# The depthwise convolution's matrix share moved to ScalarE and GpSimd, and the scan's products issued in pairs

## The chip, the cores and the metric

The kernel runs on one core of a Trainium2 chip (trn2). A core has PE (the TensorE matrix engine), VectorE (DVE in the profile), ScalarE (ACT), GpSimd (POOL) and SyncE (SP), which issues most DMAs; each works through its own list of instructions in order, and they wait for each other by semaphores. The metric is the device time of one execution in us, the median of several runs.

## The reference, cut to what matters

Three layers run over a sequence of 256 tokens with 2048 features. The change lies in the first layer, which has two branches over one projection: a depthwise convolution of 31 taps, and a grouped state-space scan.

```
proj = rmsnorm(x) @ w_in
glu  = a[:, :1024] * sigmoid(a[:, 1024:])             # a = proj[:, :2048]
y    = sum over k of w_dw[k] * padded(glu)[t + k]     # 31 taps for each of 1024 channels
y    = silu(layernorm(y + b_dw)) @ w_pw
bu   = einsum('gph,bsgh->bsgp', b_bar, ug)            # scan: 64 groups of 16 channels, 64 states
s[t] = lam_bar * s[t - 1] + bu[t]
out  = Re(c @ s) + d_skip * u ; gelu, two projections, a gate
```

...then come an output projection, a layer of retrieved experts, and a second block with a delta-rule mixer and banded attention. They are not touched.

## The kernel before

Features lie on the 128 partitions, the 256 tokens along the free dimension, so the 1024 channels of the convolution are 8 chunks of 128x256, and its input glu, its output cy and its weights dw lie in SBUF. Weights of the large products are fetched as strips of 128x1024 fp32. `strips` (L162, L163) splits a strip into wh (a ScalarE cast) and wl (a VectorE difference); `dual` (L175, L176) multiplies each by the operand, a product of 512 columns and one of 256, and `fold` (L181, L182) adds the two halves of the sum. One output block of 128 features is 16 such pairs over two strips; it is read out of PSUM by a VectorE product (`evict`, L342).

Side work is written as generators and stepped between the pairs of a block; STEP says how many steps a block takes. The scheduler then orders each engine's list, with the casts and splits of the strips at high priority, so the list differs from the order written. The first layer runs its blocks so: 8 blocks for the scan's input u, 16 blocks for glu, 32 gate blocks (about 178 to 440 us in the profile), 16 half blocks of conv_w_out, and so on.

- `ssm_scan` (L574 to L662) runs from the u blocks into conv_w_out. It handles 32 groups of two. For a group g: two fp32 products into a PSUM tile bu (L611, L612), VectorE work of 256 or 512 columns (L614 to L628), a difference and a sum of 128x256 on GpSimd (L630, L631), and three groups later the output product (`outp`, L639), which writes 32 partitions of yp. The weights of L611 and L612 have 128 rows, all but 32 of them zero. Three buffers t1 carry the groups.
- `conv` (L665 to L675) does five chunks of the convolution on VectorE, in gate blocks, one multiply-add of 128x256 for each tap and chunk (L674): first three chunks, then two.
- `conv_pe` (L704 to L736) does the other three on PE: for each tap ScalarE scales the identity twice (L728, L729) into a diagonal matrix's high and low part, and `dual` multiplies them by the split input (L722, L723): 93 pairs into cps, three folds.
- `conv_norm` (L677 to L702) follows when all eight chunks are there.

Of the kernel before, what the change touches and what calls it, by code (L numbers as in the profile page):

```python
# [10 lines left out]
F32 = mybir.dt.float32  # L11
F32R = mybir.dt.float32r
# [5 lines left out]
ALU = mybir.AluOpType  # L18
# [6 lines left out]
W2 = 512  # L25
STEP = (6, 2, 2.25, 3.7, 3, 2)
GRATE = 0.2
# [12 lines left out]
GLAG = 2  # L40
CDVE = ((0, 1, 2), (3, 4))
CPE = (5, 6, 7)
DLAG = 2
TSTEP = 2
# [72 lines left out]
class K:  # L117
# [189 lines left out]
    def mixers(self):  # L307
        nc, tc, I = self.nc, self.tc, self.I
        with ExitStack() as ctx:
# [68 lines left out]
            side = Side()  # L378
            side.add(self.ssm_scan(c1, prm, u, y, cc, wk, (sw[:, 7168:8192], cw[:, 4864:5888]), cw[:, 5888:8192]))
            evict(u[:, 2, :], p2)  # L380
# [24 lines left out]
            c4 = E(ExitStack())  # L405
            dg = c4.enter_context(tc.tile_pool(name="dg", bufs=DLAG + 1))
            side3 = Side()
            side3.add(self.conv_pe(c1, dg, glu, cy, dw, CPE))
            norm = self.conv_norm(sm, cy, *cx)
# [163 lines left out]

    def ssm_scan(self, c1, prm, u, y, cc, wk, bms, wb):  # L574

# [11 lines left out]
        tabs = [area(wk, 4 + 2 * i) for i in range(4)]  # L587
        t1s, t2s = (area(wk, 12), area(wb, 0), area(wb, 5)), (area(wk, 14), area(wb, 2), area(wb, 7))

# [12 lines left out]
        def scan(g):  # L602
            j, q = g // 4, g % 4
            t1, t2, t = t1s[g % 3], t2s[g % 3], tabs[g % 4]
            bm = bms[j % 2].rearrange("p (q k c) -> p q k c", q=4, k=2)
# [3 lines left out]
            sin = t[:, 1:2, :].to_broadcast([P, 2, T])  # L609
            bu = self.ips.tile([P, 512], F32, name="bu", tag="i").rearrange("p (k t) -> p k t", k=2)  # L610
            nc.tensor.matmul(bu[:, 0, :], lhsT=bm[:, q, 0, :], rhs=u[:, j, :], start=True, stop=True)  # L611
            nc.tensor.matmul(bu[:, 1, :], lhsT=bm[:, q, 1, :], rhs=u[:, j, :], start=True, stop=True)  # L612
            yield
            V.tensor_tensor(out=t1, in0=bu, in1=cos, op=ALU.mult)  # L614
            yield
# [18 lines left out]
        def outp(g, yp):  # L634
            q = g % 4
            t1 = t1s[g % 3]
            yo = yp[32 * q : 32 * q + 32, :]
            for n in range(2):
                nc.tensor.matmul(yo, lhsT=cc[:, g, n, :], rhs=t1[:, n, :], start=n == 0, stop=n == 1, tile_position=(0, 32 * q))  # L639

# [3 lines left out]
        for tick in range(4 * 35):  # L644
            if tick % 4 == 0:
                g = tick // 4
                if g >= 3:
                    o = g - 3
                    if o % 4 == 0:
                        yp = self.ips.tile([P, 512], F32, name="yp", tag="i")[:, :T]  # L650
                    outp(o, yp)
                    if o % 4 == 3:
                        j = o // 4
                        V.scalar_tensor_tensor(out=y[:, j, :], in0=u[:, j, :], scalar=self.vec("ssmd", j), in1=yp, op0=ALU.mult, op1=ALU.add)
                if g < 32:
                    act.append(scan(g))
                if g < 30:
                    act.append(tables(g + 2))
            for x in list(act):
                if next(x, act) is act:  # L660
                    act.remove(x)
            yield  # L662
# [40 lines left out]

    def conv_pe(self, c1, dg, glu, cy, dw, js):  # L704

        nc = self.nc
        n = js[0]
        dh = c1.tile([P, len(js), 31], F32R, name="dwh")
        nc.scalar.copy(dh, dw[:, n:, :])
        dl = c1.tile([P, len(js), 31], F32, name="dwl")  # L710
        nc.vector.tensor_tensor(out=dl, in0=dw[:, n:, :], in1=dh.bitcast(F32), op=ALU.subtract)
        late = []

        def taps(ps, d, g, j, k):
            self.dual(ps, d[0], d[1], g[:, :, k : k + T], k == 0, k == 30)
            if k == 30:
                ps = self.fold(ps)
                nc.scalar.activation(cy[:, j, :], ps, AF.Identity, bias=self.vec("cb", j))

        for j in js:  # L720
            g = dg.tile([P, 2, 30 + T], F32R, name="g", bufs=1)
            nc.scalar.copy(g[:, 0], glu[:, j, :])  # L722
            nc.vector.tensor_tensor(out=g[:, 1], in0=glu[:, j, :], in1=g[:, 0].bitcast(F32), op=ALU.subtract)  # L723
            yield
            ps = self.ips.tile([P, 512], F32, name="cps", tag="i")
            for k in range(31):
                d = [dg.tile([P, P], F32R, name="d%d" % i) for i in range(2)]
                nc.scalar.activation(d[0], self.ident, AF.Copy, scale=dh.bitcast(F32)[:, j - n, k : k + 1])  # L728
                nc.scalar.activation(d[1], self.ident, AF.Copy, scale=dl[:, j - n, k : k + 1])  # L729
                late.append((ps, d, g, j, k))  # L730
                if len(late) > DLAG:
                    taps(*late.pop(0))
                yield
            while late:
                taps(*late.pop(0))
            yield  # L736
# [1029 lines left out]
```

## Time and profile before

| what | value |
|---|---|
| median of 3 runs | 3355.14 us (3352.12 to 3356.29) |
| the profiled execution | 3351.08 us |
| its span | 3349.3 us |
| PE busy | 3291.0 us, 98% |
| VectorE busy | 2667.1 us, 80% |
| ScalarE busy | 2021.3 us, 60% |
| GpSimd busy | 171.6 us, 5% |

A profile is one execution. Busy time is the union of an engine's records; a record is longer than the distance to the next start, since instructions overlap at their ends. PE's ends are modelled. L12 stands for line 12 of the kernel. "A <- B" in a list of waits says that A's engine stood idle until B was done.

### The profile page before, as it was taken

Reading aid. Unit: us, or ns where it says so; the run is one execution under the profiler, and the core shown is the slowest. Engines: PE = TensorE matmul, PEld = TensorE weight load, DVE = VectorE, ACT = ScalarE, POOL = GpSimd, SP = SyncE. Lnnn points to the kernel's source line nnn. Section 1 sums busy time; section 2 is a strip of 40 time slices with the busy share of each in tenths; the row PEclk is TensorE's granted clock in tenths of the full one; section 3 lists DMA queues with packets and bytes.
Section 4 is the critical chain, followed back from the end, with each engine's and each line's share of the span. In section 5 each row is a group of like instructions: output and inputs, shape, how many; then the busy total and the mean of one; then the engine's idle time right before and its main releaser. Section 6 shows DMA issues by size and latency. Waiting matters only on the chain.

```text
span 3349.3 us, 53879 instructions
## 1 busy us (share of the span) xinstructions
PE 3291.0 (98%) x17962; PEld 2780.5 (83%) x17962; DVE 2667.1 (80%) x6200; ACT 2021.3 (60%) x4529; POOL 171.6 (5%) x319
## 2 busy tenths in 40 slices
PE   8999999999999999999999999999999999999999
PEld 7787778888888888888888888778888888888888
DVE  8999987789999999996555556868888768666685
ACT  6577755555555555555555556767666666566664
POOL 1211110000000000000000000000222100000000
PEclk9999999999999999999999999999999999999999
DMA  6544345765556555555666666655443436655556
GB/s 210 160 143 139 133 127 188 216 193 178 187 183 179 180 177 182 177 182 183 193 194 195 193 192 198 209 183 171 143 138 117 145 105 211 198 177 176 173 171 181
DMA packets 167655, 584.49 MB, mean 175 GB/s; under 512 B 19184, under 2 KB 25616, under 8 KB 167120
## 3 DMA queue, kind: packets, MB, share of 16 engines
q1 hardware_dynamic: 165600, 574.94, 54.8%
q0 software_dynamic: 1776, 6.10, 0.6%
q8 instruction: 141, 2.31, 0.3%
q14 instruction: 138, 1.13, 0.1%
HBM read 573.88 MB, written 7.09 MB: 173 GB/s over the span
## 4 chain that ended last, share of the span: by engine, by line
PE 90%; DVE 5%; ACT 2%; issue 1%; DMA 1%; POOL 1%; SPq 0%; ACTq 0%; DVEq 0%; POOLq 0%
PE g L175 36%; PE g L176 18%; PE va L1018 7%; PE va L1019 7%; PE va L1020 7%; PE g L1609 3%; PE g L1610 3%; PE g L1608 3%; DVE wl L163 2%; PE ip L1345 1%; ACT wh L162 1%; PE yp L639 1%; PE wp L954 1%; PE cps L175 1%; PE bu L611 1%
## 5 line engine op out<-in xcount | busy, mean ns | idle before, releaser
L162 ACT CAST wh<-raw 128x512 fp32r<-128x512 f32 (+1 forms) x1920 | 1274.2, 664 | 1080.3 <-PE g L175 553.2
L163 DVE TENSOR_TENSOR wl<-raw,wh 128x512 fp32r<-128x512 f32 (+1 forms) x1920 | 1433.8, 748 | 589.6 <-ACT wh L162 571.8
L175 PE MATMUL g<-X,wh 128*128 128x512 f32 x4752 | 1707.7, 401 | 23.0 <-ACT wh L162 8.8
L176 PE MATMUL g<-X,wl 128*128 128x256 f32 x4752 | 1337.0, 281 | 2.3 <-DVE wl L163 2.2
L175 PEld LDWEIGHTS g<-X,wh 128*128 128x128 f32 x4752 | 894.3, 188 | 234.6 <-issue 10.8
L176 PEld LDWEIGHTS g<-X,wl 128*128 128x128 f32 x4752 | 898.0, 189 | 9.9 <-DVE wl L163 5.1
L1018 PE MATMUL va<-wh,ah 128*128 128x512 f32 x1024 | 398.4, 391 | 4.5 <-DVE gg L797 2.3
L1019 PE MATMUL va<-wh,al 128*128 128x512 f32 x1024 | 400.2, 391 | 0.3 <-DVE al L1010 0.3
L1020 PE MATMUL va<-wl,ah 128*128 128x512 f32 x1024 | 399.1, 390 | 0.0
L1018 PEld LDWEIGHTS va<-wh,ah 128*128 128x128 f32 x1024 | 191.7, 188 | 46.9 <-ACT ah L1009 7.5
L1019 PEld LDWEIGHTS va<-wh,al 128*128 128x128 f32 x1024 | 192.6, 188 | 43.3 <-DVE al L1010 3.3
L1020 PEld LDWEIGHTS va<-wl,ah 128*128 128x128 f32 x1024 | 192.7, 188 | 39.7
L175 PE MATMUL g<-xo,wh 128*128 128x512 f32 x512 | 179.6, 395 | 0.0
L182 DVE TENSOR_TENSOR g<-g,fold 128x256 f32<-128x256 f32 x377 | 159.8, 424 | 4.5 <-ACT fold L181 4.0
L1608 PE MATMUL g<-wh,X 128*128 128x512 f32 x384 | 151.9, 396 | 0.0
L1610 PE MATMUL g<-wl,X 128*128 128x512 f32 x384 | 150.5, 392 | 0.0
L1609 PE MATMUL g<-wh,X 128*128 128x512 f32 x384 | 150.1, 391 | 0.0
L181 ACT COPY fold<-g 128x256 f32<-128x256 f32 x377 | 138.2, 367 | 13.5 <-DVE g L182 7.7
L176 PE MATMUL g<-xo,wl 128*128 128x256 f32 x512 | 143.6, 280 | 0.0
L944 DVE TENSOR_SCALAR oj<-iota,ijg 128x128 f16<-128x128 f16 x512 | 142.6, 307 | 0.0
L175 PEld LDWEIGHTS g<-xo,wh 128*128 128x128 f32 x512 | 96.0, 187 | 22.8 <-DVE xo L1471 0.3
L1010 DVE TENSOR_TENSOR al<-w,ah 128x256 fp32r<-128x256 f32 x256 | 106.7, 418 | 0.9 <-ACT ah L1009 0.8
(478 smaller groups left out, 3577.0 us busy)
## 6 DMA issues: line engine op xcount, KB each, us to landing
raw<-peer_u SPq DMA_DIRECT2D x256, 512.0 KB, 3.5
raw<-peer_v SPq DMA_DIRECT2D x256, 512.0 KB, 3.5
raw<-a_w_in SPq DMA_DIRECT2D x128, 512.0 KB, 3.5
raw<-w_in SPq DMA_DIRECT2D x112, 512.0 KB, 3.5
raw<-b_w_t SPq DMA_DIRECT2D x96, 512.0 KB, 3.5
raw<-w_out SPq DMA_DIRECT2D x32, 512.0 KB, 4.3
raw<-peer_w_q SPq DMA_DIRECT2D x32, 512.0 KB, 3.5
raw<-a_w_out SPq DMA_DIRECT2D x32, 512.0 KB, 3.7
```

What stands on the lines that cost most here:

```text
L162: self.marks["A"] = nc.scalar.copy(wh[:, e], raw[:, e])
L163: self.marks["V"] = nc.vector.tensor_tensor(out=wl[:, e], in0=raw[:, e], in1=wh[:, e].bitcast(F32), op=ALU.subtract)
L175: nc.tensor.matmul(pf, lhsT=wh, rhs=hl, start=start, stop=False)
L176: return nc.tensor.matmul(pf[:, :T], lhsT=wl, rhs=hl[:, 0], start=False, stop=stop)
L182: self.nc.vector.tensor_tensor(out=pf[:, :T], in0=pf[:, :T], in1=t, op=ALU.add)
L944: V.tensor_scalar(out=oj[:, k, :], in0=iota, scalar1=ijg[:, 1, t : t + 1], scalar2=ijg[:, 2 + k, t : t + 1], op0=ALU.is_equal, op1=ALU.mult)
L1018: nc.tensor.matmul(ps, lhsT=ah, rhs=wh, start=first, stop=False)
L1019: nc.tensor.matmul(ps, lhsT=al, rhs=wh, start=False, stop=False)
L1020: nc.tensor.matmul(ps, lhsT=ah, rhs=wl, start=False, stop=last)
L1608: nc.tensor.matmul(ps[a], lhsT=xh[:, k, s], rhs=wh, start=k == 0, stop=False)
L1609: nc.tensor.matmul(ps[a], lhsT=xl[:, k, s], rhs=wh, start=False, stop=False)
L1610: self.marks["P"] = nc.tensor.matmul(ps[a], lhsT=xh[:, k, s], rhs=wl, start=False, stop=k == KT - 1)
```

## The change

`conv_pe` is gone. In its place `conv_add` does four chunks (4 to 7) without PE: for each tap ScalarE multiplies the shifted input by the tap's weight (the first tap goes straight into cy, with the bias), and for the others GpSimd adds two chunks at a time to cy: 124 ScalarE instructions of 128x256 and 60 GpSimd additions of 128x512. The tap tiles come from a ring of three. `conv` keeps four chunks instead of five. A generator of 31 steps replaces one of some 100, so the fourth STEP goes from 3.7 to 1.4.

In the scan the input products of two groups are issued together, with the 32 rows of weights and input that are not zero, in the rows of the array where they lie, real parts of both groups first, then imaginary parts. The output products of two groups are issued together too, in turn, in their 32 columns each. t1 has five buffers instead of three.

```diff
-STEP = (6, 2, 2.25, 3.7, 3, 2)
+STEP = (6, 2, 2.25, 1.4, 3, 2)
-CDVE = ((0, 1, 2), (3, 4))
-CPE = (5, 6, 7)
-DLAG = 2
+CDVE = ((0, 1), (2, 3))
+CADD = (4, 6, 8)
...
-            dg = c4.enter_context(tc.tile_pool(name="dg", bufs=DLAG + 1))
+            pr = c4.enter_context(tc.tile_pool(name="pr", bufs=3))
-            side3.add(self.conv_pe(c1, dg, glu, cy, dw, CPE))
+            side3.add(self.conv_add(pr, glu, cy, dw, CADD))
...
-            bu = self.ips.tile([P, 512], F32, name="bu", tag="i").rearrange("p (k t) -> p k t", k=2)
-            nc.tensor.matmul(bu[:, 0, :], lhsT=bm[:, q, 0, :], rhs=u[:, j, :], start=True, stop=True)
-            nc.tensor.matmul(bu[:, 1, :], lhsT=bm[:, q, 1, :], rhs=u[:, j, :], start=True, stop=True)
-            yield
+            if g % 2 == 0:
+                for i in range(2):
+                    bus[g + i] = self.ips.tile([P, 512], F32, name="bu", tag="i").rearrange("p (k t) -> p k t", k=2)
+                for k in range(2):
+                    for i in range(2):
+                        r0 = 32 * (q + i)
+                        rows = slice(r0, r0 + 32)
+                        nc.tensor.matmul(bus[g + i][:, k, :], lhsT=bm[rows, q + i, k, :], rhs=u[rows, j, :], start=True, stop=True, tile_position=(r0, 0))
+            yield
+            bu = bus.pop(g)
...
             for n in range(2):
-                nc.tensor.matmul(yo, lhsT=cc[:, g, n, :], rhs=t1[:, n, :], start=n == 0, stop=n == 1, tile_position=(0, 32 * q))
+                for i in range(2):
+                    r0 = 32 * ((g + i) % 4)
+                    nc.tensor.matmul(yp[r0 : r0 + 32, :], lhsT=cc[:, g + i, n, :], rhs=t1s[(g + i) % 5][:, n, :], start=n == 0, stop=n == 1, tile_position=(0, r0))
...
-                    outp(o, yp)
+                    if o % 2 == 1:
+                        outp(o - 1, yp)
...
+    def conv_add(self, pr, glu, cy, dw, js):
...
+        for k in range(31):
+            for a, b in zip(js, js[1:]):
+                t = None if k == 0 else pr.tile([P, b - a, T], F32, name="tap")
+                for j in range(a, b):
+                    x, w = glu[:, j, k : k + T], dw[:, j, k : k + 1]
+                    if k == 0:
+                        nc.scalar.activation(cy[:, j, :], x, AF.Identity, scale=w, bias=self.vec("cb", j))
+                    else:
+                        nc.scalar.activation(t[:, j - a, :], x, AF.Copy, scale=w)
+                if k:
+                    nc.gpsimd.tensor_tensor(out=cy[:, a:b, :], in0=cy[:, a:b, :], in1=t, op=ALU.add)
             yield
```

What the scheduler makes of it stands in the engines' lists, whose line numbers after the change differ by a few. ScalarE, one early gate block before, from behind its gate's tanh (bg) to the next block's; d are the scaled identities, wh the casts of the strips, wk the scan's tables:

```order
L599 ACTIVATE wk<-wk,hpi 128x256
L181 COPY fold<-g 128x256
L728 ACTIVATE d_2127<-ident,dwh 128x128
L729 ACTIVATE d_2128<-ident,dwl 128x128
L728 ACTIVATE d_2155<-ident,dwh 128x128
L729 ACTIVATE d_2156<-ident,dwl 128x128
L162 CAST wh<-raw 128x1024
L728 ACTIVATE d_2182<-ident,dwh 128x128
L729 ACTIVATE d_2183<-ident,dwl 128x128
L162 CAST wh<-raw 128x1024
L592 ACTIVATE wk<-cw,magic,ssm_f 128x256
L419 ACTIVATE bg<-gg,hb 128x256
```

ScalarE after, the same kind of stretch a little later; tap are the convolution's products:

```order
L418 ACTIVATE bg<-gg,hb 128x256
L722 ACTIVATE tap<-cw 128x256 x6
L161 CAST wh<-raw 128x1024
L180 COPY fold<-g 128x256
L722 ACTIVATE tap<-cw 128x256 x4
L161 CAST wh<-raw 128x1024
L597 ACTIVATE wk<-wk 128x256
L722 ACTIVATE tap<-cw 128x256
L418 ACTIVATE bg<-gg,hb 128x256
```

Before, three pairs of scalings stand in a block, among the two casts; after, eleven taps do.

GpSimd before, from the sixth to the eighth group of the scan in the list; only the scan's steps stand there:

```order
L630 TENSOR_TENSOR cw<-cw 128x256
L631 TENSOR_TENSOR cw<-cw 128x256
L630 TENSOR_TENSOR wk<-wk 128x256
L631 TENSOR_TENSOR wk<-wk 128x256
L630 TENSOR_TENSOR cw<-cw 128x256
L631 TENSOR_TENSOR cw<-cw 128x256
```

GpSimd after, in the gate blocks; L636 and L637 are the scan's steps, L724 the additions to cy:

```order
L724 TENSOR_TENSOR cw<-cw,tap 128x512 x8
L636 TENSOR_TENSOR sw<-sw,cw 128x256
L637 TENSOR_TENSOR sw<-sw,cw 128x256
L724 TENSOR_TENSOR cw<-cw,tap 128x512 x10
L636 TENSOR_TENSOR sw<-sw,cw 128x256
L637 TENSOR_TENSOR sw<-sw,cw 128x256
L724 TENSOR_TENSOR cw<-cw,tap 128x512 x8
```

Eight to ten additions stand between two groups of the scan, which are two gate blocks apart; all 60 are through after some 14 of the 32 blocks.

PE before, one group of the scan between two pairs of a block (yp the output, bu the input):

```order
L176 MATMUL g<-X,wl 128x256
L639 MATMUL yp<-wk,sw 32x256 x2
L611 MATMUL bu<-sw 128x256
L612 MATMUL bu<-sw 128x256
L175 MATMUL g<-X,wh 128x512
```

PE after, two groups at once:

```order
L175 MATMUL g<-X,wl 128x256
L645 MATMUL yp<-wk,sw 32x256
L645 MATMUL yp<-cw,sw 32x256
L645 MATMUL yp<-wk,sw 32x256
L645 MATMUL yp<-cw,sw 32x256
L617 MATMUL bu<-sw,cw 128x256 x4
L174 MATMUL g<-X,wh 128x512
```

The four output and four input products of two groups now stand together. In the gate blocks the list parts some of these sets again, by up to some thirty products.

## Rows read from the trace of the kernel before

**Rows 1.** The page's shares of the span: PE's busy time, and the chain of work that ended last by engine.

```profile
PE 3291.0 (98%) x17962; PEld 2780.5 (83%) x17962; DVE 2667.1 (80%) x6200; ACT 2021.3 (60%) x4529; POOL 171.6 (5%) x319
...
PE 90%; DVE 5%; ACT 2%; issue 1%; DMA 1%; POOL 1%; SPq 0%; ACTq 0%; DVEq 0%; POOLq 0%
```

**Rows 2.** The windows of two stretches: the stretch and its length, then the busy time of PE, of PE's weight loads, of VectorE (DVE), of ScalarE (ACT) and of GpSimd (POOL), each with its count of instructions, then the granted clock of PE, the share of the DMA engines and GB/s.

```profile
40.00:178.00 138.00, 137.06 (x736) 111.03 (x735) 134.25 (x237) 85.08 (x151) 24.77 (x24) 1.00 0.52 166
178.00:440.00 262.00, 255.15 (x1385) 209.59 (x1384) 253.96 (x472) 190.66 (x424) 27.95 (x31) 0.99 0.42 136
```

**Rows 3.** The list of waits from 178 to 440 us: who waited for whom, us in all, how often, the longest in us.

```profile
DVE wl L163 <- ACT wh L162: 6.0, 9, 1.0
...
PE cps L175 <- DVE g L723: 4.3, 1, 4.3
...
PEld yp L639 <- POOL wk L630: 0.8, 1, 0.8
```

**Rows 4.** PE in time order from 186.5 to 190.2 us: start, length of the record, engine, line, operation, tiles, shape and how many in a row (one fp32 product of 256 columns is two records). The starts are what counts, since PE's ends are modelled.

```profile
186.90 1.05 PE L639 MATMUL yp<-cw,sw 128*32 128x256 f32 x4
187.88 0.70 PE L611 MATMUL bu<-sw,cw 128*128 128x256 f32 x2
...
188.66 0.58 PE L175 MATMUL g<-X,wh 128*128 128x512 f32 x1
...
189.56 0.40 PE L175 MATMUL cps<-g,d 128*128 128x512 f32 x1
...
189.91 0.40 PE L175 MATMUL g<-X,wh 128*128 128x512 f32 x1
```

**Rows 5.** VectorE in time order from 214 to 224 us, where GpSimd runs nothing: columns as in rows 4.

```profile
216.03 1.26 DVE L674 SCALAR_TENSOR_TENSOR cw<-cw 128x256 f32<-128x256 f32 x3
```

**Rows 6.** VectorE's groups of instructions from 214 to 224 us: line, operation, tiles, shapes, count, busy time, mean ns of one, idle time before them.

```profile
L674 DVE SCALAR_TENSOR_TENSOR cw<-cw 128x256 f32<-128x256 f32 x9 | 3.8, 470 | 0.0
L163 DVE TENSOR_TENSOR wl<-raw,wh 128x1024 fp32r<-128x1024 f32 x3 | 3.6, 1201 | 0.0
```

**Rows 7.** VectorE's groups of instructions from 178 to 440 us, columns as in rows 6.

```profile
L163 DVE TENSOR_TENSOR wl<-raw,wh 128x1024 fp32r<-128x1024 f32 x64 | 80.5, 1258 | 6.3 <-ACT wh L162 6.0
L674 DVE SCALAR_TENSOR_TENSOR cw<-cw 128x256 f32<-128x256 f32 x150 | 73.9, 534 | 0.0
...
L723 DVE TENSOR_TENSOR g<-cw,g 128x286 fp32r<-128x286 f32 x3 | 1.3, 443 | 0.0
L182 DVE TENSOR_TENSOR cps<-cps,fold 128x256 f32<-128x256 f32 x3 | 1.3, 421 | 0.0
```

**Rows 8.** All engines' groups from 178 to 440 us, columns as in rows 6: the identity's scalings and the scan's table step on ScalarE, and the scan's last step on GpSimd.

```profile
L729 ACT ACTIVATE d<-ident,dwl 128x128 fp32r<-128x128 f32 x93 | 36.2, 389 | 0.0
L728 ACT ACTIVATE d<-ident,dwh 128x128 fp32r<-128x128 f32 x90 | 35.7, 397 | 33.8 <-PE cps L175 33.5
...
L631 POOL TENSOR_TENSOR cw<-cw 128x256 f32<-128x256 f32 x11 | 10.8, 980 | 0.0
L630 POOL TENSOR_TENSOR cw<-cw 128x256 f32<-128x256 f32 x10 | 9.7, 968 | 142.3 <-DVE cw L628 142.3
...
L593 ACT ACTIVATE wk<-wk,magic 128x256 f32<-128x256 f32 x16 | 8.0, 502 | 0.2
...
L631 POOL TENSOR_TENSOR wk<-wk 128x256 f32<-128x256 f32 x5 | 4.4, 881 | 0.0
...
L630 POOL TENSOR_TENSOR wk<-wk 128x256 f32<-128x256 f32 x5 | 4.2, 832 | 71.2 <-DVE wk L628 71.2
```

**Rows 9.** All engines in time order from 264.5 to 268 us, columns as in rows 4.

```profile
265.29 0.85 POOL L630 TENSOR_TENSOR cw<-cw 128x256 f32<-128x256 f32 x1 [19.09 <-DVE cw L628]
...
265.47 2.24 DVE L674 SCALAR_TENSOR_TENSOR cw<-cw 128x256 f32<-128x256 f32 x3
...
266.11 0.92 POOL L631 TENSOR_TENSOR cw<-cw 128x256 f32<-128x256 f32 x1
...
267.63 0.42 DVE L182 TENSOR_TENSOR g<-g,fold 128x256 f32<-128x256 f32 x1
```

**Rows 10.** The instructions of line L163 over the whole span: count, then least, median and largest length in ns, first and last start, shapes.

```profile
L163 DVE TENSOR_TENSOR wl<-raw,wh x1920: 627/692/4017, 7.8 to 3340.1; 128x512 fp32r<-128x512 f32 x172, 128x1024 fp32r<-128x1024 f32 x20
```

**Rows 11.** All engines in time order from 2569.6 to 2570 us, columns as in rows 4: GpSimd's 128x2048 product, and the split of a strip that starts under it.

```profile
2569.71 3.67 POOL L1337 TENSOR_TENSOR xx<-tab 128x2048 f32<-128x2048 f32 x1 [2.78 <-DMA tab<-xdr]
...
2569.91 4.02 DVE L163 TENSOR_TENSOR wl<-raw,wh 128x512 fp32r<-128x512 f32 x1 [1.17 <-ACT wh L162]
```

**Rows 12.** GpSimd in time order from 459 to 461 us, where VectorE has nothing to do: columns as in rows 4.

```profile
459.35 0.74 POOL L630 TENSOR_TENSOR cw<-cw 128x256 f32<-128x256 f32 x1 [4.58 <-DVE cw L628]
460.05 0.74 POOL L631 TENSOR_TENSOR cw<-cw 128x256 f32<-128x256 f32 x1
```

**Rows 13.** PE in time order from 333 to 343 us, columns as in rows 4; in brackets the idle time ahead and what ended it.

```profile
338.70 0.79 PE L175 MATMUL cps<-g,d 128*128 128x512 f32 x1 [4.31 <-DVE g L723]
...
340.28 1.92 PE L639 MATMUL yp<-cw,sw 128*32 128x256 f32 x4
```

**Rows 14.** The windows of two shorter stretches, columns as in rows 2.

```profile
260.00:270.00 10.00, 9.04 (x48) 6.93 (x47) 10.00 (x19) 7.50 (x20) 1.74 (x2) 1.00 0.41 125
340.00:345.00 5.00, 5.00 (x21) 3.09 (x20) 5.00 (x12) 2.69 (x10) 0.18 (x1) 0.79 0.24 85
```

More of the change, by code (lines that the diff above doesn't have):

```diff
@@ L378, in mixers @@
             side = Side()
-            side.add(self.ssm_scan(c1, prm, u, y, cc, wk, (sw[:, 7168:8192], cw[:, 4864:5888]), cw[:, 5888:8192]))
+            side.add(self.ssm_scan(c1, prm, u, y, cc, wk, (sw[:, 7168:8192], cw[:, 4864:5888]), cw[:, 5888:8192], sw[:, 6144:7168]))
             evict(u[:, 2, :], p2)
@@ L572, in ssm_params, with ssm_scan @@
         return r, f2
-    def ssm_scan(self, c1, prm, u, y, cc, wk, bms, wb):
+    def ssm_scan(self, c1, prm, u, y, cc, wk, bms, wb, wc):
         nc, I = self.nc, self.I
@@ L587, in ssm_scan @@
         tabs = [area(wk, 4 + 2 * i) for i in range(4)]
-        t1s, t2s = (area(wk, 12), area(wb, 0), area(wb, 5)), (area(wk, 14), area(wb, 2), area(wb, 7))
+        t1s, t2s = (area(wk, 12), area(wb, 0), area(wb, 5), area(wc, 0), area(wc, 2)), (area(wk, 14), area(wb, 2), area(wb, 7))
+        bus = {}
         def tables(g):
@@ L603, in scan @@
             j, q = g // 4, g % 4
-            t1, t2, t = t1s[g % 3], t2s[g % 3], tabs[g % 4]
+            t1, t2, t = t1s[g % 5], t2s[g % 3], tabs[g % 4]
             bm = bms[j % 2].rearrange("p (q k c) -> p q k c", q=4, k=2)
@@ L634, in outp @@
         def outp(g, yp):
-            q = g % 4
-            t1 = t1s[g % 3]
-            yo = yp[32 * q : 32 * q + 32, :]
             for n in range(2):
-                nc.tensor.matmul(yo, lhsT=cc[:, g, n, :], rhs=t1[:, n, :], start=n == 0, stop=n == 1, tile_position=(0, 32 * q))
+                for i in range(2):
+                    r0 = 32 * ((g + i) % 4)
+                    nc.tensor.matmul(yp[r0 : r0 + 32, :], lhsT=cc[:, g + i, n, :], rhs=t1s[(g + i) % 5][:, n, :], start=n == 0, stop=n == 1, tile_position=(0, r0))
         yp = None
@@ L702, in conv_norm @@
         yield
-    def conv_pe(self, c1, dg, glu, cy, dw, js):
+    def conv_add(self, pr, glu, cy, dw, js):
         nc = self.nc
[L707 to L723, printed above, removed]
-            yield
[L725 to L735, printed above, removed]
+        for k in range(31):
[9 more added lines that the diff above has]
+                    nc.gpsimd.tensor_tensor(out=cy[:, a:b, :], in0=cy[:, a:b, :], in1=t, op=ALU.add)
             yield
```

## The prediction

> **What bounds the kernel now.** I read the busy shares first, then the windows of the stage that the change touches, then what waits for what there, then single instructions in time order.
>
> The chain that ended last is 90% PE, and PE is 98% busy [rows 1]. Averages over the whole span don't tell what a change in one stage is worth, so the second view is the windows. The reader is to see in them that in the 262 us of the gate blocks (178 to 440 us) PE is busy for 255 us and VectorE for 254 us: two engines stand at 97% at once [rows 2]. In the list of waits of that stretch VectorE's wait for wh is 6.0 us in all, while PE's largest single wait is 4.3 us, for the input split of L723, which VectorE delivered late [rows 3]. So here PE's loss of work is worth only what VectorE can follow: VectorE idles for 262 - 254 = 8 us. From 40 to 178 us PE is busy for 137.1 of 138 us and VectorE for 134.3 us [rows 2], a slack of 3.7 us. Behind 520 us nothing is changed.
>
> **PE's part.** The removed diagonal products are 93 pairs. A pair stands 0.35 us apart from the next start (189.56 to 189.91 us) [rows 4], so 93 x 0.35 = 32.5 us leave PE, and PE needs about 255 - 32.5 = 223 us in the stage. The scan's products of one group take 186.90 to 187.88 us for the output and 187.88 to 188.66 us for the input [rows 4], 1.76 us together, 56 us over 32 groups. No row here shows two products at once in different rows or columns, so I bound the packing: 0 if each pass still waits for the last, half (28 us) if two run at once. Where PE sets the pace (40 to 178 us, some 12 groups) that is 0 to 12 x 0.88 = 10.6 us, capped by VectorE's slack of 3.7 us; I take 2 us. In the gate blocks PE is no longer what ends last, and the packing is worth nothing there. The order also splits some pairs there (one yp ahead of a bu, the rest blocks later), which changes PE alone. The Trainium skill (TensorE: Matmul & The Clock Gate, Part 3) says that products in different row or column groups run at once and a pack lasts about as long as one of them; by it the 2 us would be 3.7 us, and no run here shows it yet.
>
> **VectorE's part, removed.** One chunk of five leaves: 31 instructions of L674. Three in a row undisturbed take 1.26 us [rows 5] where one takes 0.47 us [rows 6], so they start 0.395 us apart and their records overlap by 0.075 us: 31 x 0.395 = 12.3 us. The three splits L723 and the three folds of cps (0.44 and 0.42 us recorded [rows 7], 0.075 us less each from start to start) make 2.1 us. VectorE's list shrinks by 14.4 us, to 254 - 14.4 = 240 us.
>
> **ScalarE's part.** 186 scalings of the identity (0.39 us each [rows 8]) go and 124 taps of 128x256 come; the nearest row is L593 with 0.50 us [rows 8]. That is 72 us out and 62 us in, on an engine that is busy for 191 of 262 us [rows 2]: hidden. The order matters more. The taps are spent in about 14 gate blocks instead of the program's 23, five to eleven a block, with the casts wh behind them, and every second tap waits for a buffer of the ring of three, that is for GpSimd. GpSimd takes the scan's steps L630 and L631 in turn with up to ten additions, and the output products on PE wait for them; before, that wait was 0.8 us at most in the stage [rows 3].
>
> **GpSimd's part, added.** 60 additions of 128x512, both operands in SBUF. This is the term that decides. The rows to see are those at 265 us: GpSimd's L630 and L631 (128x256) run while VectorE has three conv instructions queued; these three take from 265.47 to 267.63 us, 2.16 us instead of 3 x 0.395 = 1.19 us [rows 9]. So two short additions cost VectorE 0.97 us, 0.49 us each. Does the cost grow with the length of the addition? The 128x2048 instruction L1337 lasts 3.67 us, and a wl of 128x512 (median 0.69 us [rows 10]) that starts under it takes 4.02 us: 3.33 us lost [rows 11]. Between 0.49 us for 256 elements and 3.33 us for 2048 the straight line gives 0.49 + 256/1792 x 2.84 = 0.90 us for 512.
>
> Not every addition meets a VectorE instruction that minds it. In the stage the 150 conv instructions have a mean of 534 ns and the 64 wl one of 1258 ns [rows 7]; from 214 to 224 us, where GpSimd adds nothing, the means are 470 and 1201 ns [rows 6]. So 150 x 0.064 + 64 x 0.057 = 13.2 us go to the 31 short additions [rows 8], 0.43 us each, 87% of 0.49 us. I take the same share: 0.87 x 0.90 = 0.78 us, so 60 x 0.78 = 47 us. The bounds: 60 x 0.43 = 26 us if a long addition costs no more than a short one, 60 x 0.90 = 54 us if each hits in full; and nothing if VectorE holds other work each time, which the same rows speak against.
>
> The Trainium skill (SBUF — State Buffer, Who interferes with whom) goes further: the first to start holds the shared pair for its whole instruction and the other blocks fully. An addition alone takes 0.70 to 0.74 us (459.35 to 460.05 us) [rows 12], yet costs VectorE 0.49 us, so the trace agrees in kind and not in size. By the whole instruction, some 1.15 us for 512 elements on the line from 0.74 to 3.67 us, the sum would be 60 x 1.15 = 69 us in place of 47 us.
>
> **The sum.** VectorE's list in the gate blocks: 254 - 14.4 + 47 = 287 us. I leave its 8 us of idle time: the wait for wh may shrink as PE runs ahead, and may grow as the casts stand behind taps. The stage becomes 295 us, +33 us; the packing gives 2 us back ahead of it. Scan and norm behind 440 us keep their instructions: 0. The profiled execution took 3351.1 us (span 3349.3 us): 3351.1 + 33 - 2 = 3382 us. It lies 4.1 us under the median of the three runs, 3355.1 us, so the forecast is 3386 us.
>
> **The rivals.**
>
> *Faster: the additions are hidden.* If GpSimd finds the shared path free when VectorE reads PSUM, or VectorE passes first and GpSimd waits, the cost is 0. Then VectorE's 240 us are the end (PE 223 us, ScalarE less): 22 us gained, 3.7 us more ahead of it, 3355 - 26 = 3329 us. For it: PE leads the chain that ended last [rows 1], and it loses 32.5 us. Against it: the rows at 265 us. Chance 0.18.
>
> *No change: a long addition costs like a short one, and VectorE's idle time goes.* 26 - 14.4 - 8 - 2 = +2 us: 3357 us. It needs both: with the idle time kept it is 3365 us, at the near end of the forecast. Speaks for it: half of 128x512 may pass while VectorE is between instructions. Against: 3.33 us under L1337. Chance 0.12.
>
> *Slower still: ScalarE is held by GpSimd, and the clock falls.* The taps stand ahead of the casts wh on ScalarE; a tap waits for an addition three back, that addition stands behind a scan step L630, and this waits for VectorE. If this chain leaves PE idle for long, its clock falls: after the wait that ended at 338.70 us (4.3 us) the mean granted clock was 0.79 from 340 to 345 us (the 1.2 GHz level for a part of it), and four output passes took 1.92 us instead of 1.05 us [rows 4, 13, 14]. Ten such falls, 5 x 0.21 = 1.0 us each, and the full 54 us in place of 47 us make +17 us: 3403 us. It decides where PE's gaps pass those seen without a fall, 1.0 us of idle time from 260 to 270 us (clock 1.00) [rows 14]. The rule of the whole instruction gives 69 - 47 = +22 us, 3408 us, as a mechanism of its own; both share a chance of 0.20.
>
> *The packing does nothing.* It moves the forecast by 2 us and decides nothing; it is inside the likeliest case.
>
> **How the numbers follow.** The likeliest case, 3386 us with 3367 to 3395 us, has 0.50; slower still 0.20; no change 0.12; faster 0.18. A measurement of this kernel can tell about 0.2%, 7 us, from no change. So faster 0.18, same 0.12, slower 0.70. The likeliest case's range follows from a cost per addition of 0.60 us with the idle time gone (36 - 14.4 - 8 - 2 = +12 us) to 0.90 us with it kept (54 - 14.4 - 2 = +38 us). For 8 in 10 the range goes from 3338 us (half of the faster case is left out) to 3412 us, past both slower cases (some 0.06 is left out above).
>
> **What would show it.** Right: in the profile after, conv instructions of the conv (L674 before) with a mean well over 534 ns in the gate blocks, wl over 1258 ns, VectorE still at 95% of a stage of some 290 us, PE at about three quarters, and 60 additions of 1.2 to 1.6 us with no long wait of ScalarE. Wrong: VectorE's instructions at their undisturbed length under an addition; or VectorE idle for more than 20 us, which would put the chain ScalarE–GpSimd in its place; or yp and bu products that start together, with a gain from 40 to 178 us beyond 4 us.

## The result, and the profile after

The changed kernel takes 3387.09 us (median of 4 runs, 3379.16 to 3389.94) beside 3353.80 us for the kernel before (median of 4 runs): a ratio of 1.0095, 95% interval 1.0074 to 1.0115. It is slower by 33 us, where 31 us were forecast. The profiled execution took 3379.16 us with a span of 3377.4 us, 28.1 us more than the one before. Line numbers have moved: wl is now L162 (L163 before), the read-out of a block L341 (L342), the conv instruction L681 (L674); the new tap is L722 and the new addition L724.

The first view is the windows, cut where those of before were cut [rows 2], with two more behind. The columns are busy us (and instructions) of PE, PEld, DVE, ACT, POOL, then the granted clock, the DMA share and GB/s.

```profile
core 0: us, PE busy (x) PEld busy (x) DVE busy (x) ACT busy (x) POOL busy (x), PEclk, DMA share, GB/s
40.00:178.00 138.00, 133.04 (x750) 106.22 (x748) 137.53 (x237) 89.20 (x159) 33.47 (x27) 1.00 0.51 167
178.00:440.00 262.00, 210.51 (x1029) 165.16 (x1029) 259.02 (x363) 155.78 (x295) 120.61 (x83) 0.92 0.39 124
440.00:480.00 40.00, 33.20 (x185) 25.11 (x183) 37.86 (x82) 29.95 (x62) 5.80 (x6) 0.91 0.29 91
480.00:520.00 40.00, 35.20 (x180) 27.00 (x180) 35.49 (x64) 18.19 (x37) 8.60 (x8) 0.96 0.39 127
```

The reader is to see one engine at its end in place of two: VectorE is busy for 259.0 of 262 us, PE for 210.5 us. VectorE does 363 instructions in the time in which it did 472 before. The gate blocks, from the start of the first read-out gg to that of the last, take 288.1 us (191.6 to 479.7 us) where they took 256.3 us (190.1 to 446.4 us). The page's chain that ended last is still mostly PE (84%, VectorE 9%; 90% and 5% in [rows 1]): the average over 3377 us tells little of this stage.

The groups of instructions from 178 to 440 us (shapes, count, busy us and mean ns of one, idle time before them) tell why:

```profile
L724 POOL TENSOR_TENSOR cw<-cw,tap 128x512 f32<-128x512 f32 x57 | 94.5, 1674 | 45.2 <-ACT tap L722 44.9
L162 DVE TENSOR_TENSOR wl<-raw,wh 128x1024 fp32r<-128x1024 f32 x59 | 80.6, 1366 | 3.0 <-ACT wh L161 2.9
L681 DVE SCALAR_TENSOR_TENSOR cw<-cw 128x256 f32<-128x256 f32 x117 | 77.8, 700 | 0.0
L722 ACT ACTIVATE tap<-cw 128x256 f32<-128x256 f32 x111 | 50.1, 498 | 3.0 <-POOL cw L724 3.0
L181 DVE TENSOR_TENSOR g<-g,fold 128x256 f32<-128x256 f32 x28 | 11.8, 421 | 0.0
```

The conv instruction has a mean of 700 ns (534 in [rows 7]), wl one of 1366 ns (1258); a tap costs ScalarE 498 ns (0.50 was forecast) and hardly waits for GpSimd (3.0 us in all). The waits of the same stretch (us in total, times, longest):

```profile
POOL cw L724 <- ACT tap L722: 44.9, 23, 6.5
PE g L174 <- DVE gg L341: 28.4, 13, 5.5
PE g L175 <- DVE wl L162: 12.4, 7, 3.0
ACT tap L722 <- POOL cw L724: 3.0, 4, 1.4
DVE wl L162 <- ACT wh L161: 2.9, 5, 0.8
```

PE waits for VectorE (28.4 and 12.4 us), GpSimd for ScalarE, and VectorE for next to nothing. How an addition meets VectorE is seen in time order (start and length in us; a row with x2 is two instructions back to back). First VectorE, then GpSimd:

```profile
237.78 1.22 DVE L162 TENSOR_TENSOR wl<-raw,wh 128x1024 fp32r<-128x1024 f32 x1
238.92 1.77 DVE L634 TENSOR_TENSOR cw<-cw,wk 128x512 f32<-128x512 f32 x1
240.61 1.51 DVE L626 TENSOR_TENSOR wk<-wk 128x256 f32<-128x256 f32 x1
...
272.75 0.41 DVE L341 TENSOR_TENSOR gg<-g,rstd 128x256 f32<-128x256 f32 x1
273.08 2.30 DVE L162 TENSOR_TENSOR wl<-raw,wh 128x1024 fp32r<-128x1024 f32 x1
```

```profile
238.02 3.82 POOL L724 TENSOR_TENSOR cw<-cw,tap 128x512 f32<-128x512 f32 x2 [0.83 <-ACT tap L722]
...
273.02 1.28 POOL L724 TENSOR_TENSOR cw<-cw,tap 128x512 f32<-128x512 f32 x1 [1.28 <-ACT tap L722]
```

The wl that began at 237.78 us, ahead of the addition, keeps its undisturbed 1.22 us, and the two additions behind it take 3.82 us together. L634 and L626, which come after, take 1.77 and 1.51 us where they take 0.68 and 0.41 us undisturbed: 1.09 and 1.10 us lost. At 273 us the addition is first by 0.06 us, keeps its 1.28 us, and wl loses 1.09 us (2.30 for 1.21). So a full meeting costs 1.09 us.

To sum this up I take as undisturbed the length that three in ten of a kind of VectorE instruction don't exceed, and add what the others have beyond it, where that is over 12%. Over 40 to 520 us this sum, the excess in what follows, is 73.3 us, and before 18.0 us. The 60 additions account for 55.3 us, 0.92 us each (0.78 was forecast).

### The profile page after: what moved, and what is told of

It reads as the page before. It is cut to its first block, busy times and chain, and to the rows that moved or that the text cites. A ratio compares the mean times of both kernels' runs of the same rounds, so it can differ in the third digit from the quotient of the medians.

```text
span 3377.4 us, 53511 instructions
## 1 busy us (share of the span) xinstructions
PE 3264.4 (97%) x17776; PEld 2752.6 (82%) x17776; DVE 2706.2 (80%) x6162; ACT 2015.2 (60%) x4459; POOL 278.6 (8%) x379
## 4 chain that ended last, share of the span: by engine, by line
PE 84%; DVE 9%; ACT 3%; issue 2%; DMA 1%; POOL 1%; DVEq 0%; SPq 0%; ACTq 0%; POOLq 0%
PE g L174 33%; PE g L175 17%; PE va L1007 7%; PE va L1008 7%; PE va L1009 7%; DVE wl L162 4%; PE g L1598 3%; PE g L1599 3%; PE g L1597 3%; PE ip L1334 2%; ACT wh L161 1%; DVE cw L681 1%; PE wp L943 1%; DVE g L181 0%; DVE wk L595 0%
## 5 line engine op out<-in xcount | busy, mean ns | idle before, releaser
L162 DVE TENSOR_TENSOR wl<-raw,wh 128x512 fp32r<-128x512 f32 (+1 forms) x1920 | 1444.1, 753 | 576.7 <-ACT wh L161 557.8
L174 PE MATMUL g<-X,wh 128*128 128x512 f32 x4752 | 1718.2, 404 | 64.3 <-DVE gg L341 28.4
L174 PEld LDWEIGHTS g<-X,wh 128*128 128x128 f32 x4752 | 904.1, 190 | 284.4 <-issue 28.6
L175 PEld LDWEIGHTS g<-X,wl 128*128 128x128 f32 x4752 | 909.1, 191 | 34.1 <-DVE wl L162 28.0
L181 DVE TENSOR_TENSOR g<-g,fold 128x256 f32<-128x256 f32 x377 | 160.5, 426 | 4.3 <-ACT fold L180 4.0
```

What stands on the lines that cost most here:

```text
L162: self.marks["V"] = nc.vector.tensor_tensor(out=wl[:, e], in0=raw[:, e], in1=wh[:, e].bitcast(F32), op=ALU.subtract)
L174: nc.tensor.matmul(pf, lhsT=wh, rhs=hl, start=start, stop=False)
L175: return nc.tensor.matmul(pf[:, :T], lhsT=wl, rhs=hl[:, 0], start=False, stop=stop)
L181: self.nc.vector.tensor_tensor(out=pf[:, :T], in0=pf[:, :T], in1=t, op=ALU.add)
```

## The experiments

My theory was the forecast's: about 0.8 to 0.9 us of VectorE time for each addition, and little from the pairs. Its rivals were that another part of the change makes the time (the order, the taps on ScalarE), and that the additions cost by number, not by size.

**The pairs alone.** The scan of the changed kernel, the convolution of before.

```diff
-            t1, t2, t = t1s[g % 3], t2s[g % 3], tabs[g % 4]
+            t1, t2, t = t1s[g % 5], t2s[g % 3], tabs[g % 4]
...
-            nc.tensor.matmul(bu[:, 0, :], lhsT=bm[:, q, 0, :], rhs=u[:, j, :], start=True, stop=True)
...
+                        nc.tensor.matmul(bus[g + i][:, k, :], lhsT=bm[rows, q + i, k, :], rhs=u[rows, j, :], start=True, stop=True, tile_position=(r0, 0))
...
-                nc.tensor.matmul(yo, lhsT=cc[:, g, n, :], rhs=t1[:, n, :], start=n == 0, stop=n == 1, tile_position=(0, 32 * q))
+                    nc.tensor.matmul(yp[r0 : r0 + 32, :], lhsT=cc[:, g + i, n, :], rhs=t1s[(g + i) % 5][:, n, :], start=n == 0, stop=n == 1, tile_position=(0, r0))
```

> The kernel before with the scan of the kernel after: products in pairs, five t1 buffers, the convolution as before (five chunks on VectorE, three on PE). Theory (VectorE's list is the end from 40 to 440 us, its slack there 3.7 us and 8 us): 0 to -8 us, some -3 us, though bu and yp of two groups start together. Rival (PE is the end): the packed products give PE up to 28 us back, -15 to -28 us. Rival (packing does nothing, or its waits for two groups cost more): 0 to +10 us.

Measured: 3343.40 us, ratio 0.9971 (0.9958 to 0.9983), 11 us faster: more than expected. PE in time order shows the pairs:

```profile
104.34 0.40 PE L646 MATMUL yp<-cw,sw 128*32 128x256 f32 x1
104.34 0.40 PE L646 MATMUL yp<-sw 128*32 128x256 f32 x1
104.58 0.38 PE L646 MATMUL yp<-cw,sw 128*32 128x256 f32 x1
104.58 0.38 PE L646 MATMUL yp<-sw 128*32 128x256 f32 x1
...
105.32 1.13 PE L618 MATMUL bu<-sw,cw 32*128 32x256 f32 x8
106.39 0.51 PE L175 MATMUL g<-X,wh 128*128 128x512 f32 x1
```

The passes of two groups start in the same 10 ns, 0.21 to 0.24 us from pair to pair. The output passes of both groups take 104.34 to 105.32 us, 0.98 us, as long as one group's took (186.90 to 187.88 us [rows 4]). With the input passes two groups take 104.34 to 106.39 us, 2.05 us, where they took 2 x 1.76 us = 3.52 us [rows 4]: 42% less. From 68 to 190 us the scan's products take 13.4 us of PE, and 21.8 us before (104 and 100 passes, from first start to the next other product). Of these 8.4 us the glu blocks gave 2.8 us to the time (their last read-out starts at 178.0 us, 180.8 us before), since VectorE is busy for 136.1 of 138 us there; the gate blocks gave 3.8 us more (252.5 us for 256.3), and what lies from the last gate block to the scan's last product another 2.7 us (29.5 for 32.2). The window of the gate blocks shows where their part comes from:

```profile
178.00:440.00 262.00, 249.81 (x1404) 203.33 (x1403) 258.97 (x478) 193.25 (x430) 34.70 (x32) 0.99 0.44 138
```

VectorE's idle time falls from 8.0 us [rows 2] to 3.0 us: PE gets its share done sooner, and VectorE waits less.

**The additions alone.** The changed kernel with the scan of before.

```diff
-            t1, t2, t = t1s[g % 5], t2s[g % 3], tabs[g % 4]
+            t1, t2, t = t1s[g % 3], t2s[g % 3], tabs[g % 4]
...
+            nc.tensor.matmul(bu[:, 0, :], lhsT=bm[:, q, 0, :], rhs=u[:, j, :], start=True, stop=True)
+            nc.tensor.matmul(bu[:, 1, :], lhsT=bm[:, q, 1, :], rhs=u[:, j, :], start=True, stop=True)
...
```

> The kernel after with the scan of the kernel before: the convolution on ScalarE and GpSimd, products one group at a time. Theory: PE is not the end in the gate blocks, so the time is that of the kernel after within 5 us, some +30 to +38 us over the kernel before. Rival (the packing brings a loss of its own, its waits for two groups): 10 us or more under the kernel after. Rival (packing was a gain that hid part of the cost): 10 us or more over it.

Measured: 3395.57 us, ratio 1.0126 (1.0109 to 1.0143), 41 us slower. It is 8.5 us over the changed kernel, between what was expected (within 5 us) and the rival (10 us or more); the pairs are worth about as much beside the additions as alone.

```profile
178.00:440.00 262.00, 211.67 (x1005) 164.38 (x1004) 253.98 (x351) 150.76 (x287) 121.75 (x86) 0.92 0.36 121
```

VectorE is busy for 254.0 of 262 us from 178 to 440 us, as before, so its idle time is the same 8 us, and its records exceed their undisturbed length by 74.1 us, 56.1 us more than before: 56.1 less the 14.4 us of removed instructions is 41.7 us, and 40.8 us were measured. PE's removed products brought nothing that this sum would miss.

**The additions almost without reading.** Each addition becomes one of 8 columns and an iota over the other 248; the sums of chunks 4 to 7 are left out, and what follows takes the iota's numbers.

```diff
-                    nc.gpsimd.tensor_tensor(out=cy[:, a:b, :], in0=cy[:, a:b, :], in1=t, op=ALU.add)
+                    nc.gpsimd.tensor_tensor(out=cy[:, a:b, 0:8], in0=cy[:, a:b, 0:8], in1=t[:, :, 0:8], op=ALU.add)
+                    nc.gpsimd.iota(cy[:, a:b, 8:T], pattern=[[T, b - a], [1, T - 8]], base=0, channel_multiplier=0, allow_small_or_imprecise_dtypes=True)
```

> The kernel after, each GpSimd addition replaced by an addition of 8 of its 256 columns and an iota that writes the other 248: the sums of chunks 4 to 7 are left out, GpSimd still has 60 places in the same order, still takes the taps and frees their ring. Theory (VectorE waits for additions that read SBUF): the 50 us vanish, VectorE's list is 14 us shorter than before, -10 to -25 us against the kernel before. Rival (the order: taps ahead of casts, scan steps behind GpSimd's list, ring of three): the waits stay, +15 us or more against the kernel before.

Measured: 3350.08 us, ratio 0.9984 (0.9975 to 0.9994), 5 us faster; less than expected. The excess over undisturbed length falls from 73.3 to 20.8 us, so the cost does hang on the additions' operands. But VectorE is not full then. Window and wait from 178 to 440 us:

```profile
178.00:440.00 262.00, 229.34 (x1184) 181.12 (x1185) 244.39 (x435) 177.29 (x343) 79.10 (x125) 0.94 0.41 137
```

```profile
DVE wl L162 <- ACT wh L161: 20.1, 15, 4.9
```

VectorE idles for 17.6 us by the window, and the list of waits puts nearly all of it down to the cast wh (20.1 us in 15 waits, the first of them begun ahead of the window; 6.0 us before [rows 3]). In time order, 11 of the 14 that begin in the window (10.4 of 15.2 us) end with a cast for which ScalarE itself had stood idle until a PE product was done, and three (4.8 us) with a cast right behind a tap. So additions that cost nothing would not have brought the 26 us of the faster rival either.

**Additions where nothing else changes.** The kernel before with 60 more additions of 128x512 on GpSimd, whose sums go nowhere. In the first form nothing tied them to their place.

```diff
...
+                        nc.gpsimd.tensor_tensor(out=xa[:, 0], in0=xa[:, 0], in1=xa[:, 1], op=ALU.add)
...
```

> The kernel before with 60 GpSimd additions of 128x512 more, on unused memory that nobody waits for, two per gate block and step. No tap, no chunk and no product is moved. Theory: each costs VectorE 0.78 to 0.92 us, so +45 to +57 us against the kernel before; less where VectorE's idle time takes some up, not under +35 us. Rival (the order and the waits of the moved work are the cost, contention is small): 0 to +15 us. By the rule that an addition holds the path for its whole length (some 1.15 us): +69 us.

Measured: 3410.54 us, ratio 1.0167 (1.0150 to 1.0184), but they ran from 0 to 100 us: the u blocks end at 122 us where they ended at 67 us. The place was missed, and the size proves nothing for the gate blocks. In the second form each pair of additions reads gate tiles, and so stands in the gate blocks:

```diff
+                if 0 < j < 31:
+                    for _ in range(2):
+                        nc.gpsimd.tensor_tensor(out=xa, in0=xa, in1=gt[:, j - 1 : j + 1, :], op=ALU.add)
```

> The kernel before with 60 GpSimd additions of 128x512 more, two behind each of 30 gate blocks: each adds two finished gate tiles to unused memory, so none can run ahead of its block, and nobody on the path waits for them. Theory: 0.78 to 0.92 us of VectorE each, +40 to +57 us against the kernel before, its instructions of L674 and L163 longer by that. Rival (contention is small, the moved order is the cost): 0 to +15 us.

Measured: 3405.07 us, ratio 1.0150 (1.0133 to 1.0167): 51.6 us, 0.86 us for each addition. Nothing leaves PE or VectorE here, no tap is on ScalarE, and the scan is that of before. The window of 178 to 440 us, and its groups of the conv instruction (L679 here) and of the addition:

```profile
178.00:440.00 262.00, 222.31 (x1145) 177.08 (x1144) 254.19 (x382) 158.88 (x361) 108.92 (x76) 0.97 0.35 113
...
L679 DVE SCALAR_TENSOR_TENSOR cw<-cw 128x256 f32<-128x256 f32 x142 | 100.1, 746 | 0.0
...
L424 POOL TENSOR_TENSOR sw<-sw,bg 128x512 f32<-128x512 f32 x48 | 82.3, 1715 | 130.8 <-ACT bg L421 129.0
```

A mean of 746 ns where it was 534 [rows 7], and an excess over undisturbed length of 68.6 us, 50.7 us more than before: 0.84 us an addition. This is the cost by itself, at a granted clock of 0.97 where the changed kernel has 0.92.

**Half of the additions.** The changed kernel without taps 1 to 30 of chunks 6 and 7 (30 additions and 60 taps fewer; those sums are left out).

```diff
+                if k and a == 6:
+                    continue
...
-                if k:
+                if k and a == 4:
```

> The kernel after with the taps 1 to 30 of chunks 6 and 7 left out: 60 ScalarE taps and 30 GpSimd additions fewer, VectorE's and PE's work as in the kernel after. Theory: 30 x 0.92 = 27 us less, some +6 us against the kernel before; if the removed ones leave VectorE idle, as with the additions that only write, some 20 us less. Rival (a full GpSimd or ScalarE queue, which gives way at a threshold): over 40 us less, or under 10 us.

Measured: 3364.94 us, ratio 1.0032 (1.0020 to 1.0045), 22 us under the changed kernel: 0.74 us for each addition left out. The excess falls by 24.6 us, 0.82 us each.

**The same sums in short additions.** 120 additions of 128x256 in place of 60 of 128x512.

```diff
-CADD = (4, 6, 8)
+CADD = (4, 5, 6, 7, 8)
```

> The changed kernel with 120 additions of 128x256 (one chunk each) in place of 60 of 128x512; the sum is the same. Theory (the price grows with the elements): two short additions cost VectorE 2 x 0.43 to 0.49 us = 0.86 to 0.98 us, one long one 0.92 us in the changed kernel, so the time stays within 6 us of the changed kernel's 3387 us. Rival (a price per instruction): twice as many instructions cost up to 55 us more, 3440 us; or, if each begins and ends between two VectorE instructions more often, 20 us less.

Measured: 3377.93 us, ratio 1.0070 (1.0053 to 1.0087), 9 us under the changed kernel, a little beyond what was expected, on the side of the lower cost. The price by number (3440 us) falls. The excess is 62.7 us, 44.7 us over that of before: 0.37 us for 256 columns, 0.92 us for 512.

**The additions on VectorE.** The changed kernel with its 60 additions on VectorE.

```diff
-                    nc.gpsimd.tensor_tensor(out=cy[:, a:b, :], in0=cy[:, a:b, :], in1=t, op=ALU.add)
+                    nc.vector.tensor_tensor(out=cy[:, a:b, :], in0=cy[:, a:b, :], in1=t, op=ALU.add)
```

> The kernel after with its 60 additions of 128x512 on VectorE in place of GpSimd. VectorE's undisturbed instruction of that shape on two SBUF operands starts 0.60 us after the last one, so its list grows by 36 us and loses the 55 us of waits under additions. Theory: 15 to 25 us under the kernel after (+8 to +18 us against the kernel before). Rival (GpSimd takes work off VectorE, contention is the smaller part): at least 10 us over the kernel after.

Measured: 3382.70 us, ratio 1.0087 (1.0071 to 1.0104), 4 us under the changed kernel, whose own runs lie 11 us apart: no difference that these runs can tell. Both expectations missed. The window and two waits from 178 to 440 us, and the additions' group:

```profile
178.00:440.00 262.00, 209.23 (x1036) 165.77 (x1034) 248.17 (x424) 158.17 (x298) 26.98 (x28) 0.90 0.37 125
```

```profile
DVE wl L162 <- ACT wh L161: 13.6, 16, 2.2
PE g L174 <- ACT wk L597: 12.4, 4, 4.1
```

```profile
L724 DVE TENSOR_TENSOR cw<-cw,tap 128x512 f32<-128x512 f32 x60 | 40.0, 698 | 0.0
```

The excess falls by 51.3 us (73.3 to 22.0), the additions take 40.0 us, and VectorE's idle time in this window grows by 10.9 us (259.0 to 248.2 us busy). 51.3 - 40.0 - 10.9 = 0.4 us, and 4 us were measured. So an addition costs VectorE 0.67 us when it does it itself, 0.92 us when GpSimd does it; what that would have won went into the wait for wh. The expectation of the next run puts that wait down to the taps ahead of the cast. The trace shows another cause: before each of the 16 casts that VectorE waited for, ScalarE itself stood idle until a PE product was done. The longest of these waits, in time order on PE, ScalarE and VectorE, with the window of PE's stretch between:

```profile
276.01 0.77 PE L174 MATMUL g<-X,wh 128*128 128x512 f32 x1 [4.14 <-DVE gg L341]
...
276.60:281.00 4.40, 4.40 (x15) 3.77 (x14) 3.56 (x8) 1.01 (x3) 0.00 (x0) 0.50 0.02 9
...
281.29 1.05 ACT L161 CAST wh<-raw 128x1024 fp32r<-128x1024 f32 x1 [3.68 <-PE g L174]
...
282.37 1.23 DVE L162 TENSOR_TENSOR wl<-raw,wh 128x1024 fp32r<-128x1024 f32 x1 [2.21 <-ACT wh L161]
```

PE had waited 4.14 us for VectorE's read-out gg; behind it the granted clock is 0.50 (the 1.2 GHz level), and a pair takes 0.64 us in place of 0.35. So the product that the cast waits for comes late. Of the 13.6 us, 9.7 us come behind casts in whose last 5 us PE took over 0.5 us a pair for at least 1 us. Here the lower clock does reach VectorE. The next run spreads the taps over more blocks:

```diff
-STEP = (6, 2, 2.25, 1.4, 3, 2)
+STEP = (6, 2, 2.25, 1.0, 3, 2)
```

> The additions on VectorE, and the generator of the taps stepped at 1.0 instead of 1.4 a block, so that there are about a fifth more casts among the taps on ScalarE's list. Theory: with the additions on VectorE its idle time (13.8 us in 178 to 440 us, nearly all of it for a cast behind taps) takes half of what the end of the contention gives; thinner taps shrink it, 3 to 8 us less than 3383 us. Rival: the idle time has another cause, or the later end of the sums delays the norm: no change or more.

Measured: 3382.74 us, ratio 1.0080 (1.0063 to 1.0097), no change from 3382.70 us. VectorE's wait for wh is 11.7 us in place of 13.6 us, and 9.6 us of it again follow a PE product. The run weighs more than the taps: the last addition starts at 456.6 us (394.6 us without the spread), so the convolution's norm comes behind the gate blocks. These are shorter, 274.5 us for 291.6, but from the last of them to the scan's last product it takes 48.8 us for 28.7. The rival named this later end. A deeper ring of tap tiles was not tried.

**A better division.** Pairs, and the convolution's chunks four on VectorE and four on PE, no taps.

```diff
-STEP = (6, 2, 2.25, 3.7, 3, 2)
+STEP = (6, 2, 2.25, 4.8, 3, 2)
...
-CDVE = ((0, 1, 2), (3, 4))
-CPE = (5, 6, 7)
+CDVE = ((0, 1), (2, 3))
+CPE = (4, 5, 6, 7)
```

> The scan in pairs, the convolution without GpSimd: four chunks on VectorE, four on PE as diagonal products (fourth STEP 4.8). Against the pairs alone VectorE loses 12.3 us, PE gains 31 x 0.35 = 10.9 us, ScalarE 24 us. Theory (pairs alone left both near their limit): within -8 and +8 us of the pairs alone, -2 to -18 us against the kernel before. Rival (VectorE alone is the end in the pairs): -10 us or more against the pairs alone.

Measured: 3334.43 us, ratio 0.9940 (0.9923 to 0.9957): 19 us under the kernel before, the fastest of all, and 9 us under the pairs alone, a little beyond what was expected. The window from 178 to 440 us:

```profile
178.00:440.00 262.00, 259.16 (x1505) 216.49 (x1503) 249.59 (x461) 217.29 (x508) 38.83 (x35) 1.00 0.43 142
```

The time that the pairs free on PE (259.2 us busy) takes the fourth chunk, and VectorE has 249.6 us to do where the pairs alone left it 259.0 us. The gate blocks take 244.5 us (188.6 to 433.1 us). The four and four chunks without the pairs were not run.

**The scan's difference and sum on VectorE.** In the kernel with the pairs alone, then in the better division.

```diff
-            nc.gpsimd.tensor_tensor(out=t1[:, 0, :], in0=t1[:, 0, :], in1=t2[:, 1, :], op=ALU.subtract)
-            nc.gpsimd.tensor_tensor(out=t1[:, 1, :], in0=t1[:, 1, :], in1=t2[:, 0, :], op=ALU.add)
+            V.tensor_tensor(out=t1[:, 0, :], in0=t1[:, 0, :], in1=t2[:, 1, :], op=ALU.subtract)
+            V.tensor_tensor(out=t1[:, 1, :], in0=t1[:, 1, :], in1=t2[:, 0, :], op=ALU.add)
```

> The kernel before with the scan issued in pairs, and the scan's last difference and sum (two of 128x256 a group) on VectorE instead of GpSimd. Theory: on VectorE they cost 2 x 0.335 us a group, 0.67 us; on GpSimd they cost VectorE 0.43 us (mean) to 0.49 us each, 0.86 to 0.98 us a group. So 0 to 10 us less than the pairs alone (3343 us): taking work off VectorE in this way saves nothing. Rival (the move to GpSimd pays, as it takes 21 us off VectorE over 32 groups): 10 to 20 us more than the pairs alone.

> The version with pairs and four convolution chunks on each of VectorE and PE, and the scan's last step on VectorE as well. Theory: as for the pairs with the scan's step on VectorE, 0 to 8 us less than without it (3334 us), since VectorE is still busy for 249.6 of 262 us in the gate blocks. Rival: PE, at 259.2 of 262 us, is now what ends last, and the time stays within 3 us of 3334 us; or the move to GpSimd pays and it is 10 to 20 us more.

Measured: 3351.13 us (ratio 0.9990, 0.9981 to 1.0000) and 3342.48 us (0.9961, 0.9947 to 0.9975), each about 8 us over the version without the edit. The theory's number missed. With no addition left on GpSimd, VectorE's excess is 0.0 us in both (20.7 and 15.4 us without the edit), so GpSimd is the only source of it; 64 instructions of some 0.34 us add about 22 us, and the list comes out even. In the gate blocks, where VectorE is full, the edit does pay a little: they take 249.8 us for 252.5, and 240.2 us for 244.5 in the better division. The loss lies ahead of them: the glu blocks' last read-out starts at 189.6 us for 178.0, and at 187.3 us for 180.1. There the edit's order breaks PE's pairs up. In the pairs alone the glu blocks hold six whole packs of 16 passes, here three, and PE in time order shows pieces:

```profile
140.39 0.62 PE L646 MATMUL yp<-cw,sw 128*32 128x256 f32 x2
140.94 0.69 PE L618 MATMUL bu<-sw 32*128 32x256 f32 x2
141.57 0.39 PE L176 MATMUL g<-X,wl 128*128 128x256 f32 x1
```

Two passes take 0.55 and 0.63 us from start to start, where a whole pack of 16 has 2.05/8 = 0.26 us for two. The scan takes 18.8 us of PE from 68 to 190 us, 13.4 us in the pairs alone. That these 5.4 us are the whole loss is not shown. So the two runs do not weigh GpSimd against VectorE by themselves.

## Why the prediction was right, and where it was off

- **What bounds.** Right. PE's removed 32.5 us bring nothing, as VectorE is the end: 259.0 of 262 us, PE waiting for it; with the additions alone VectorE's terms make 41.7 us, and 40.8 us were measured.
- **The term of the additions.** Right in mechanism: the extra additions in the gate blocks cost 51.6 us by themselves, and half of the dose takes 22 us away. By the records it was 8 us too small, 0.92 us an addition for 0.78 us; the two runs give 0.86 and 0.74 us. The straight line from 256 to 2048 columns gave 0.90 us for a full meeting, and the rows show 1.09 us; the share of meetings, 87%, was near (0.92/1.09 = 84%). A full meeting costs an addition's length less 0.2 to 0.3 us: 1.09 of 1.28 us here, 0.49 of 0.72 us and 3.33 of 3.67 us before [rows 9, 11, 12].
- **The rule of the whole instruction.** The Trainium skill (SBUF — State Buffer, Who interferes with whom) says that the first to start holds the shared pair for its whole instruction. It is nearer than the forecast said: a full meeting costs 85% of the addition's length (1.09 of 1.28 us). The forecast's 69 us by it did not come: not every addition meets an instruction that minds it. L181, which reads PSUM, keeps 421 ns on average in a stage full of additions, and L341 its 0.41 us.
- **The pairs.** Mis-sized: 2 us forecast, 8.5 us beside the additions and 11 us alone. The step that failed is not the cap in the glu blocks (2.8 us there) but "in the gate blocks the packing is worth nothing" and "behind 440 us: 0". Without the pairs the gate blocks with the additions take 293.5 us, with them 288.1 us, and the stretch to the scan's last product 31.3 and 28.6 us. The reading that one engine ends a stage at every moment was too coarse: VectorE at 97% still waits for casts that wait for PE, and a shorter PE step takes up some of that idle time.
- **VectorE's idle time.** Left at 8 us in the forecast, it did stay at 8 us with the additions alone, and fell to 3 us with the pairs. These 5 us are part of what the pairs are worth, not a term beside them.
- **The sum.** -14.4 + 55.3 - 8.5 = +32 us; the medians differ by 33 us, the profiled executions by 28.1 us. Forecast: -14.4 + 47 - 2 = +31 us. The misses of +8 and -6.5 us nearly cancel; that the number is so near is luck, though its terms are of the right kind. The 8.5 us are the difference of two runs, so what this sum tests is the part of the additions. The 14.4 us were not measured by themselves. The likeliest range's upper end of 3395 us is 2 us over its own sum (3355 + 38 us).
- **ScalarE held by GpSimd, and the clock.** The first is not so: 3.0 us. Late casts are real once the additions cost nothing (20.1 us of waits) or stand on VectorE (13.6 us), but most of them wait for PE; in the changed kernel VectorE waits 2.9 us for them, as it is late itself. The granted clock did fall (0.92 in the stage, 0.99 before), where PE waits for VectorE anyway. The additions cost much the same at 0.97 (added to the kernel before), and without their reads the time is under that of before at 0.94. So the additions' cost does not hang on the fall.

## What to carry to other kernels

When two engines share a stage at 97% each, price an edit by what it does to both of them, and ask what the third engine, off the path, does to their operands: an elementwise step given to GpSimd beside a full VectorE cost VectorE 0.92 us, and 0.67 us when VectorE did it, though the whole time hardly differed. Measure such a cost by adding the suspected instructions to the old kernel, tied to their place, before moving anything. When a change has two parts, time them apart: the pairs were worth 11 us, and with the work rebalanced between PE and VectorE 19 us, under a change that was slower as a whole.

## What the runs showed of the hardware

- fp32 products of two groups in different rows or columns of the array start within 10 ns of each other, and two groups need 2.05 us where they need 3.52 us in turn, 58%. A pack broken up into twos loses this again: 0.55 to 0.63 us for two passes between other products.
- GpSimd's additions and VectorE's SBUF instructions take turns, whoever is first: the later one waits, and the addition's own record grows from 1.28 to 1.67 us on average. VectorE instructions that read PSUM keep their length (421 ns and 0.41 us). With no addition left on GpSimd the excess is 0.0 us: GpSimd is its only source here.
- After PE had waited 4.14 us for VectorE, its granted clock was 0.50 for the next 4.4 us and a pair took 0.64 us in place of 0.35; the cast behind it came late, and VectorE idled 2.21 us.
- An instruction of GpSimd that only writes (iota, 0.55 us each) costs VectorE little: the excess is 20.8 us with 60 of them and 60 small additions, and 18.0 us in the kernel before.
